# A transformer layer on one core: the blocks of the Strassen stage are split in one piece each, two masks and scores share their buffers with it, a bias is loaded ahead, and the last third product is gated ahead

## The chip, the cores and the metric

The kernel runs on one core of one Trainium2 chip. The core has a matrix engine (TensorE, in the profile PE, with its weight loads as PEld), a vector engine (VectorE, DVE), an activation engine (ScalarE, ACT), GpSimd (POOL) and a queue engine (SyncE, SP), and 16 DMA engines. The metric is the time of one execution on the device in microseconds (us); less is better. Before the change it is 780.21 us, the median of three runs from 778.95 to 781.56.

## The reference

One layer over 512 tokens of width 1024 in f32: an RMS norm whose scale and shift come from a second input `c`, two causal sparse attentions, a gated merge, an output projection, and a gated feed-forward part of inner width 2816. The change lies in the last part, and in the gate vector `gt_f` that multiplies it:

```python
mod = jax.nn.silu(c) @ w_mod[l] + b_mod[l]
sh_m, sc_m, gt_m, sh_f, sc_f, gt_f = [m[:, None, :] for m in jnp.split(mod, N_MOD, axis=-1)]
...
h = rms_norm(x, g_ffn_norm[l]) * (1.0 + sc_f) + sh_f
g_ff, u_ff = jnp.split(h @ w_gate_up[l], 2, axis=-1)
x = x + gt_f * ((jax.nn.silu(g_ff) * u_ff) @ w_down[l])
```

## The kernel before

**Numbers.** Every f32 matmul operand is split into a high part (a cast to a rounded f32 form, on ACT) and a low part (value minus high part, a subtraction on DVE). A product is three matmuls: high by high, high by low, low by high (`mm3`).

**Order.** The kernel is written as tasks. While it is built, a planner keeps a clock for each engine, holds the free times of every buffer in `free`, and issues the instructions of PE, ACT, DVE and POOL in the order that its clocks, the `slack` and the `rank` of a task give; that order is final. Each of these engines works through its own queue in order. All of these instructions pass one helper, so the profile gives them all line L110. DMAs issued by SP have lines of their own: L183 weights of the earlier stages, L1012 the bias rows, L1408 and L1423 `w_down`, L1446 the stored sums, L1486 and L1523 the output. POOL issues DMAs at L1245 (`pool_dma`). Buffers are named by tags: `st` holds arriving weights (three buffers), `H`, `O`, `K`, `wh`/`wl` hold high and low parts, `s`, `gu`, `pT`, `cg`, `g` hold f32 blocks, `psacc`, `pstr`, `pspv`, `pss` are accumulators.

**Gate vector.** `gtf_task` makes `gt_f` in two halves of 512 columns. For each half `mod_rows` lets DVE sum the rows of `w_mod` weighted by silu(c) into `cg` (SCALAR_TENSOR_TENSOR on `st`), makes its high part on ACT (`gu<-cg`) and its low part on DVE (`gu<-cg,gu`), then loads the bias over `cg` itself (L1012), sums over the partitions with two matmuls by a column of ones (`pstr<-gu,oner`), and adds the bias on DVE (`cg<-pstr,cg`). This runs beside the first matmuls of the gate and up projection.

**Down projection.** It is one level of Strassen's scheme in Winograd's form. The 2816 rows of `w_down` are 11 pairs of 256 rows (NPAIR = 11, here c0 to c10), and for each pair the weights are four blocks of 128 x 512. In the first half a pair gives 24 matmuls of 128x512: products M1, M6, M7, M5, each for two token tiles. `load_first_half` fetches two blocks in one `st` and a third in `pT` or `gu`; `split_first_half` forms three sums on DVE (T3, T2, T1), of which T2 goes to a buffer `s` and by POOL to memory, and `split_into` makes high and low parts, the pair of blocks in `st` as one 128x1024 operation. `homes` gives the buffers for the parts: by turns `wh`/`wl` or two `H`. Pair 10's activations are finished while c0 and c1 are multiplied (`s<-psacc`, `gu<-s`, then low parts `O<-s`, `O<-gu`). In the second half a pair gives 18 matmuls (M2, M3, M4), with block T4 formed from the stored sum (`gu<-st,gu` or `pT<-st,pT`); `second_task` brings half of each pair's activations back from memory into `O` or `K`. Pairs 9 and 10 come together in `end`.

**Output.** `shared_sums` and `share` add up the products that several output blocks share and gate them (`g<-g,cg`, then `V<-V,g`) during the second half. `settle` multiplies a finished accumulator by `gt_f` into `s`, adds it to the residual `V` and stores a block. At the end M4's accumulators are settled: the first token tile as 128x512, the second in two pieces of 256 columns in new accumulators.

Of the kernel before, what the change touches and what calls it, by code (L numbers as in the profile page):

```python
# [116 lines left out]
def layer(ctx, tc, x, vecs, w_mod, w_in, gvecs, w_br_dsa, w_br_moba, w_out, w_gate_up, w_down, cosh, sinh, cosi, sini, out):  # L117
# [11 lines left out]
    NB = {"H": 4, "O": 4, "K": 4, "V": 2, "g": 16, "gu": 2, "s": 3, "pT": 2, "cg": 2}  # L129
# [101 lines left out]
    cmask = cp.tile([P, S], F32, name="cmask")  # L231
# [577 lines left out]
    def index_queries(i):  # L809
# [22 lines left out]
        sc = cp.tile([P, w], F32, name=f"score{i}")  # L832
# [45 lines left out]
    def head(br, i, h):  # L878
# [46 lines left out]
        if not any(b == br for b, _, _ in heads):  # L925
            ready.add(f"attn{br}")
            done(vals["vb" if br else "va"], qk["qb" if br else "qa"], qk["kb" if br else "ka"])

# [78 lines left out]
    def mod_rows(acc, col0, tag):  # L1007

        yield from column_sums(col0, tag, acc)
        parts = yield from halves(acc)  # L1010
        r0 = 24 + col0 // P
        nc.sync.dma_start(acc.rearrange("p (a d) -> p a d", d=P), vecs[r0:r0 + 4].partition_broadcast(P))  # L1012
        arriving(acc, 512)
        yield parts + (room("pstr"), acc)
# [3 lines left out]
        ve.tensor_tensor(out=acc, in0=pg, in1=acc, op=ALU.add)  # L1018
        done(pg, *parts)

# [346 lines left out]
    def gtf_task():  # L1367
        yield "ffn0"
        for half in range(2):
            yield room("cg")  # L1370
            gtf.append(t("cg", [P, 512]))
            yield from mod_rows(gtf[half], 5 * D + half * 512, "st")
        ready.add("gtf")
# [37 lines left out]

    def block_tag():
# [14 lines left out]
    def split_first_half(loaded):  # L1427

        c, st, b = loaded
        yield st, b, room("s")  # L1430
        t2 = t("s", [P, 512])
        ve.tensor_tensor(out=b, in0=b, in1=st[:, 1], op=ALU.subtract)
        ve.tensor_tensor(out=t2, in0=b, in1=st[:, 0], op=ALU.add)
        ve.tensor_tensor(out=st[:, 1], in0=st[:, 1], in1=st[:, 0], op=ALU.subtract)
# [3 lines left out]
        places = [(h0, l0), (h1[:, 0], l1[:, 0]), (h1[:, 1], l1[:, 1])]  # L1438
        yield from split_into(places, [(st, st), (b, b), (t2, t2)])
        pool_dma(sums2[c], t2, out_of=t2)  # L1440
        done(st, b, t2)
        return {"B11": (h0[:, 0], l0[:, 0]), "T1": (h0[:, 1], l0[:, 1]), "T3": places[1], "T2": places[2]}, tiles
# [7 lines left out]
    def split_second_half(loaded):  # L1450
# [3 lines left out]
        ve.tensor_tensor(out=b, in0=st[:, 0], in1=b, op=ALU.subtract)  # L1454
        places, tiles = yield from homes(3)
# [18 lines left out]
    def settle(i, half, acc, cs=slice(0, 512), store=True):  # L1474

        pump(lambda: "gtf" in ready)
        need_room("s")
        tmp = t("s", [P, 512])
# [226 lines left out]
```

## Time and profile before

| | us |
|---|---|
| median of the runs | 780.21 |
| the profiled execution's own time | 780.61 |
| its span in the trace | 778.8 |
| PE busy in the span | 764.0 (98%) |
| DVE busy | 542.8 (70%) |
| ACT busy | 390.8 (50%) |
| POOL busy | 48.2 (6%) |

Of the profiled execution 1.8 us lie outside the span. Busy time of an engine is summed over its instructions; idle time is put down to the instruction whose semaphore came last. A row of the timeline has the start of a run of like instructions, their time together, the engine, the line, the operation, the tiles and a count, and in brackets the idle time before and what ended it. The granted clock is TensorE's: 1.00 is 2.4 GHz, and in a stretch with a lower number part of the time was at 1.2 GHz.

### The profile page before, as it was taken

To read this page: it belongs to the slowest core of one execution; us is meant where nothing else is said; L and a number is where in the kernel's file an instruction comes from. 1 tells how busy PE (TensorE), PEld (TensorE's weight loads), DVE (VectorE), ACT (ScalarE), POOL (GpSimd) and SP (SyncE) were. 2 spreads that over 40 slices of the span, in tenths; PEclk is the share of its full clock that TensorE was granted. 3 is DMA by queue.
4 is the path that set the end of the run, shared out by engine and by line. 5 is a ranking of instruction groups with operands and counts; after the bars stand their busy time and mean duration, and the time that the engine had idled before them with its cause. 6 is when DMAs were issued, how large, how long until landed. Compare 5 with 4: busy or idle time off the path is not lost.

```text
span 778.8 us, 10322 instructions
## 1 busy us (share of the span) xinstructions
PE 764.0 (98%) x3668; PEld 633.6 (81%) x3668; DVE 542.8 (70%) x1023; ACT 390.8 (50%) x824; POOL 48.2 (6%) x65
## 2 busy tenths in 40 slices
PE   7999999999999999999999999999999999899997
PEld 6887888888788878888889987788888888788886
DVE  6974889989699786248768257554544446897787
ACT  6763786779776747624446223233332233444340
POOL 2000012001111000000000000000000000111100
PEclk9999999999999999999999999999999999999999
DMA  9976352531135364334521186543334444489882
GB/s 310 339 227 221 84 180 71 182 108 55 52 87 197 98 216 150 123 108 148 168 90 30 54 257 208 184 134 127 106 120 149 140 131 166 167 278 354 307 294 82
DMA packets 84560, 126.60 MB, mean 163 GB/s; under 512 B 8976, under 2 KB 49240, under 8 KB 84508
## 3 DMA queue, kind: packets, MB, share of 16 engines
q1 hardware_dynamic: 80460, 105.75, 42.5%
q0 software_dynamic: 4048, 20.19, 7.7%
q8 instruction: 29, 0.48, 0.3%
q14 instruction: 23, 0.19, 0.1%
HBM read 112.28 MB, written 13.64 MB: 162 GB/s over the span
## 4 chain that ended last, share of the span: by engine, by line
PE 93%; DVE 2%; SPq 2%; DMA 1%; issue 1%; ACT 0%; ACTq 0%; DVEq 0%
PE psacc L110 60%; PE pstr L110 15%; PE pspv L110 9%; PE pss L110 8%; SPq L183 1%; DMA K<-in_w_mod_dram 1%; DVE s L110 1%; DMA cg<-in_vecs_dram 1%; SPq L212 0%; DVE V L110 0%; DVE H L110 0%; DVE O L110 0%; ACT H L110 0%; SPq L221 0%; DVE gu L110 0%
## 5 line engine op out<-in xcount | busy, mean ns | idle before, releaser
L110 PE MATMUL psacc<-H,wh 128*128 128x512 f32 x576 | 182.7, 398 | 0.0
L110 DVE TENSOR_TENSOR wl<-st,wh 128x1024 fp32r<-128x1024 f32 (+1 forms) x106 | 127.8, 1206 | 61.1 <-ACT wh L110 58.3
L110 ACT CAST wh<-st 128x1024 fp32r<-128x1024 f32 (+1 forms) x106 | 109.6, 1035 | 88.0 <-PE psacc L110 32.6
L110 PE MATMUL psacc<-wh,H 128*128 128x512 f32 x384 | 126.4, 400 | 0.9 <-ACT H L110 0.9
L110 PEld LDWEIGHTS psacc<-H,wh 128*128 128x128 f32 x576 | 106.0, 188 | 22.3 <-issue 2.1
L110 PE MATMUL psacc<-H,wl 128*128 128x512 f32 x288 | 112.4, 390 | 0.0
L110 PEld LDWEIGHTS psacc<-wh,H 128*128 128x128 f32 x384 | 72.0, 188 | 16.4 <-ACT H L110 1.4
L110 PE MATMUL psacc<-wl,H 128*128 128x512 f32 x192 | 71.0, 390 | 0.0
L110 PEld LDWEIGHTS psacc<-H,wl 128*128 128x128 f32 x288 | 54.1, 188 | 11.6
L110 PE MATMUL pstr<-H,wh 128*128 128x512 f32 (+1 forms) x176 | 54.4, 390 | 1.7 <-DVE cg L110 1.7
L110 POOL TENSOR_TENSOR m<-m,mhalf 128x4 f32<-128x4 f32 (+1 forms) x24 | 28.6, 1192 | 390.9 <-DVE m L110 357.0
L110 PEld LDWEIGHTS psacc<-wl,H 128*128 128x128 f32 x192 | 36.1, 188 | 6.8
L110 PEld LDWEIGHTS pstr<-H,wh 128*128 128x128 f32 (+1 forms) x176 | 32.2, 183 | 9.7 <-DVE cg L110 2.2
L110 PE MATMUL psacc<-O,wh 128*128 128x512 f32 x128 | 39.4, 389 | 0.0
L110 ACT ACTIVATE s<-s,att 128x256 f32<-128x256 f32 (+3 forms) x64 | 34.2, 562 | 4.0 <-DVE att L110 3.7
L110 PE MATMUL psacc<-H,O 128*128 128x256 f32 (+1 forms) x240 | 35.4, 305 | 0.0
L110 PE MATMUL pstr<-H,wl 128*128 128x512 f32 (+1 forms) x88 | 34.3, 390 | 0.0
L110 DVE TENSOR_TENSOR s<-psacc,s 128x512 f32<-128x512 f32 x12 | 8.3, 690 | 37.3 <-PE psacc L110 34.7
L110 PEld LDWEIGHTS psacc<-H,O 128*128 128x128 f32 x240 | 32.1, 191 | 1.9
L110 ACT CAST H<-st 128x1024 fp32r<-128x1024 f32 x14 | 14.8, 1055 | 34.7 <-PE psacc L110 26.7
L110 PEld LDWEIGHTS psacc<-O,wh 128*128 128x128 f32 x128 | 24.0, 188 | 5.0
L110 PE MATMUL psacc<-wh,K 128*128 128x512 f32 x82 | 26.1, 389 | 0.0
(290 smaller groups left out, 1442.7 us busy)
## 6 DMA issues: line engine op xcount, KB each, us to landing
st<-in_w_gate_up_dram SPq DMA_DIRECT2D x88, 256.0 KB, 3.6
st<-in_w_in_dram SPq DMA_DIRECT2D x36, 512.0 KB, 3.6
K<-in_w_mod_dram SPq DMA_DIRECT2D x12, 1024.0 KB, 6.4
st<-in_w_down_dram SPq DMA_DIRECT2D x22, 512.0 KB, 4.8
second<-O POOLq DMA_DIRECT2D x11, 768.0 KB, 5.3
K<-in_w_mod_dram SPq DMA_DIRECT2D x16, 512.0 KB, 6.1
K<-second POOLq DMA_DIRECT2D x6, 768.0 KB, 7.5
st<-in_w_in_dram SPq DMA_DIRECT2D x16, 256.0 KB, 4.2
```

Of the source, the lines that this page charges most:

```text
L110: inst = f(*args, **kw)
L183: last_dma[0] = nc.sync.dma_start(st[:, :, o:o + n], src.rearrange("(k p) n -> p k n", p=P))
```

## The change

- `split_first_half` no longer calls `split_into`. It issues, for each pair, the cast of the first block, the three sums in the order T3, T1, T2, the other three casts, and right behind, after one `yield`, the four low parts, each 128x512; the 128x1024 cast and subtraction become two of half the size. T2 may go to `sc` or `s`.
- A new tag `sc` with two buffers holds the causal mask and the scores of the last token tile, and, when attention is over, biases and T2.
- `mod_rows` with a `bias_tag` takes a buffer `sc` for the bias and loads it before the column sums; `gtf_task` uses it. The matmuls wait for the planner's time of the low part plus 1.0.
- For c9 and c10 `split_second_half` multiplies T4 by the first half of `gt_f`, so M4 of these pairs comes out gated. M4 of c0 to c8 is settled with a product as before, for both token tiles, after c8; the last M4 gets an accumulator of its own and `settle(..., gated=True)` adds it to `V` in one operation.
- `share` tasks get slack 3.0 and rank 2, `second_task` slack 8.0 and rank 0.

```diff
@@ -126,7 +126,7 @@
     pp = ctx.enter_context(tc.tile_pool(name="pp", bufs=1, space=PS))
     dp = ctx.enter_context(tc.tile_pool(name="dp", bufs=1, space=bass.MemoryType.DRAM))
 
-    NB = {"H": 4, "O": 4, "K": 4, "V": 2, "g": 16, "gu": 2, "s": 3, "pT": 2, "cg": 2}
+    NB = {"H": 4, "O": 4, "K": 4, "V": 2, "g": 16, "gu": 2, "s": 3, "pT": 2, "cg": 2, "sc": 2}
     uid = [0]
     last_dma = [None]
 
...
@@ -829,7 +829,7 @@
         yield tuple(qT)
         kT = idx["kT"]
         w = (i + 1) * P
-        sc = cp.tile([P, w], F32, name=f"score{i}")
+        sc = t("sc", [P, w]) if i == NT - 1 else cp.tile([P, w], F32, name=f"score{i}")
 
         def weigh(h, rl):
             if h == 0:
...
@@ -1004,19 +1006,29 @@
         landed[0] = max(ck.dma, ck.ready[sums.tensor.name][0]) + 9.0
         done(tile)
 
-    def mod_rows(acc, col0, tag):
-
+    def mod_rows(acc, col0, tag, bias_tag=None):
+
+        r0 = 24 + col0 // P
+
+        def load_bias(tile):
+            nc.sync.dma_start(tile.rearrange("p (a d) -> p a d", d=P), vecs[r0:r0 + 4].partition_broadcast(P))
+            arriving(tile, 512)
+
+        if bias_tag:
+            yield room(bias_tag)
+            load_bias(bias := t(bias_tag, [P, 512]))
         yield from column_sums(col0, tag, acc)
         parts = yield from halves(acc)
-        r0 = 24 + col0 // P
-        nc.sync.dma_start(acc.rearrange("p (a d) -> p a d", d=P), vecs[r0:r0 + 4].partition_broadcast(P))
-        arriving(acc, 512)
-        yield parts + (room("pstr"), acc)
+        if not bias_tag:
+            load_bias(bias := acc)
+        yield parts + (room("pstr"), bias, lambda: ck.ready[parts[1].tensor.name][0] + 1.0)
         pg = ps("tr")
         for n, part in enumerate(parts):
             te.matmul(pg, oner.to_broadcast([P, P]), part, start=n == 0, stop=n == 1)
-        ve.tensor_tensor(out=acc, in0=pg, in1=acc, op=ALU.add)
+        ve.tensor_tensor(out=acc, in0=pg, in1=bias, op=ALU.add)
         done(pg, *parts)
+        if bias_tag:
+            done(bias)
 
     gtm = []
     landed = [0.0]
@@ -1369,7 +1381,7 @@
         for half in range(2):
             yield room("cg")
             gtf.append(t("cg", [P, 512]))
-            yield from mod_rows(gtf[half], 5 * D + half * 512, "st")
+            yield from mod_rows(gtf[half], 5 * D + half * 512, "st", "sc")
         ready.add("gtf")
 
 
@@ -1409,6 +1421,9 @@
         arriving(st, 1024)
         return st
 
+    def earliest(*tags):
+        return lambda: min([min(free[tag]) for tag in tags if free[tag]], default=None)
+
     def block_tag():
 
         tags = [tag for tag in ("pT", "gu") if free[tag] and (tag == "pT" or f"stored{NPAIR - 1}" in ready)]
@@ -1427,19 +1442,26 @@
     def split_first_half(loaded):
 
         c, st, b = loaded
-        yield st, b, room("s")
-        t2 = t("s", [P, 512])
-        ve.tensor_tensor(out=b, in0=b, in1=st[:, 1], op=ALU.subtract)
-        ve.tensor_tensor(out=t2, in0=b, in1=st[:, 0], op=ALU.add)
-        ve.tensor_tensor(out=st[:, 1], in0=st[:, 1], in1=st[:, 0], op=ALU.subtract)
+        yield st, b, earliest("sc", "s")
+        t2 = t(min((tag for tag in ("sc", "s") if free[tag]), key=lambda tag: min(free[tag])), [P, 512])
         sums2[c] = dp.tile([P, 512], F32, name=f"sums{c}")
         places, tiles = yield from homes(4)
         (h0, l0), (h1, l1) = places
-        places = [(h0, l0), (h1[:, 0], l1[:, 0]), (h1[:, 1], l1[:, 1])]
-        yield from split_into(places, [(st, st), (b, b), (t2, t2)])
+        places = [(h0[:, 0], l0[:, 0]), (h0[:, 1], l0[:, 1]), (h1[:, 0], l1[:, 0]), (h1[:, 1], l1[:, 1])]
+        blocks = [st[:, 0], st[:, 1], b, t2]
+
+        se.copy(places[0][0], blocks[0])
+        ve.tensor_tensor(out=b, in0=b, in1=st[:, 1], op=ALU.subtract)
+        ve.tensor_tensor(out=st[:, 1], in0=st[:, 1], in1=st[:, 0], op=ALU.subtract)
+        ve.tensor_tensor(out=t2, in0=b, in1=st[:, 0], op=ALU.add)
+        for n in (2, 1, 3):
+            se.copy(places[n][0], blocks[n])
+        yield
+        for n in (0, 2, 1, 3):
+            ve.tensor_tensor(out=places[n][1], in0=blocks[n], in1=places[n][0].bitcast(F32), op=ALU.subtract)
         pool_dma(sums2[c], t2, out_of=t2)
         done(st, b, t2)
-        return {"B11": (h0[:, 0], l0[:, 0]), "T1": (h0[:, 1], l0[:, 1]), "T3": places[1], "T2": places[2]}, tiles
+        return dict(zip(("B11", "T1", "T3", "T2"), places)), tiles
 
     def load_second_half(c):
         st, b = rows_of(2 * c + 1), t(block_tag(), [P, 512])
@@ -1452,6 +1474,9 @@
         c, st, b = loaded
         yield st, b
         ve.tensor_tensor(out=b, in0=st[:, 0], in1=b, op=ALU.subtract)
+        if c >= NPAIR - 2:
+
+            ve.tensor_tensor(out=b, in0=b, in1=gtf[0], op=ALU.mult)
         places, tiles = yield from homes(3)
         (h0, l0), (h1, l1) = places
         places = [(h0, l0), (h1[:, 0], l1[:, 0])]
@@ -1471,17 +1496,20 @@
             pair_tiles[q] = [x]
             ready.add(f"second{q}")
 
-    def settle(i, half, acc, cs=slice(0, 512), store=True):
-
-        pump(lambda: "gtf" in ready)
-        need_room("s")
-        tmp = t("s", [P, 512])
+    def settle(i, half, acc, cs=slice(0, 512), gated=False, store=True):
+
         n = cs.stop - cs.start
-        ve.tensor_tensor(out=tmp[:, :n], in0=acc[:, :n], in1=gtf[half][:, cs], op=ALU.mult)
         cols = slice(half * 512 + cs.start, half * 512 + cs.stop)
         xs = x1[i // 2][:, i % 2, cols]
-        ve.tensor_tensor(out=xs, in0=xs, in1=tmp[:, :n], op=ALU.add)
-        done(tmp)
+        if gated:
+            ve.tensor_tensor(out=xs, in0=xs, in1=acc[:, :n], op=ALU.add)
+        else:
+            pump(lambda: "gtf" in ready)
+            need_room("s")
+            tmp = t("s", [P, 512])
+            ve.tensor_tensor(out=tmp[:, :n], in0=acc[:, :n], in1=gtf[half][:, cs], op=ALU.mult)
+            ve.tensor_tensor(out=xs, in0=xs, in1=tmp[:, :n], op=ALU.add)
+            done(tmp)
         if store:
             nc.sync.dma_start(ov[:, i, cols], xs)
 
@@ -1508,7 +1536,7 @@
             ve.tensor_tensor(out=c12, in0=acc, in1=kept["U2", tt], op=ALU.add)
             ve.tensor_tensor(out=c22, in0=acc, in1=kept["U3", tt], op=ALU.add)
             done(kept["U2", tt])
-            spawn(share(tt, c12, c22, kept["U3", tt]), slack=1.0, rank=3, on=(DVE,))
+            spawn(share(tt, c12, c22, kept["U3", tt]), slack=3.0, rank=2, on=(DVE,))
 
     def share(tt, c12, c22, u3):
         yield "gtf"
@@ -1565,7 +1593,7 @@
                 settle(tt, 1, acc)
             else:
                 pump(lambda: f"shared{tt}" in ready)
-                settle(2 + tt, 0, acc, store=tt == 0)
+                settle(2 + tt, 0, acc, store=False)
             if n != "M1":
                 done(acc)
 
...
@@ -1596,11 +1624,19 @@
                 for tt in range(2):
                     if (n, tt) == ("M4", 1):
                         continue
+                    if n == "M4":
+                        need_room("psacc")
+                        banks[n, tt] = ps("acc")
                     for q in (last - 1, last):
                         emptied_next[0] = q == last
-                        product(n, a, b, tt, q, held, q == last, banks[n, tt], skip=n == "M2")
+                        product(n, a, b, tt, q, held, q == last, banks[n, tt], start=n == "M4" and q != last,
+                                skip=n == "M2")
                     emptied_next[0] = False
-                    finish(n, tt)
+                    if n == "M4":
+                        settle(2 + tt, 0, banks[n, tt], gated=True)
+                        done(banks[n, tt])
+                    else:
+                        finish(n, tt)
                     step()
 
             n, a, b, _ = table[-1]
@@ -1610,7 +1646,7 @@
                 cs = slice(e, e + 256)
                 for q in (last - 1, last):
                     product(n, a, b, 1, q, held, q == last, acc, cs=cs, start=q != last, more=False)
-                settle(3, 0, acc, cs=cs)
+                settle(3, 0, acc, cs=cs, gated=True)
                 done(acc)
             leave(last - 1, last)
 
...
@@ -1652,7 +1689,7 @@
         for k2 in range(NK // 2):
             spawn(resident("w0", w0, gate_up_src(0, k2), 2, w0_hl, "attn0", "attn1", room("O")))
         spawn(gtf_task())
-        spawn(second_task())
+        spawn(second_task(), slack=8.0, rank=0, on=(DVE,))
         dve = (DVE,)
         spawn(columns_task(), slack=1.0, rank=3, on=dve)
         for i in range(1, NT):
```

The instructions of DVE in the first half, where c2 and c3 are split. In the kernel before, `pT_5969` and `st_5967` are c2's blocks, `pT_6029` and `st_6027` c3's, and the `O` rows are pair 10's activations:

```order
L110 TENSOR_TENSOR pT_5969<-pT_5969,st_5967 128x512
L110 TENSOR_TENSOR s_6064<-pT_5969,st_5967 128x512
L110 TENSOR_TENSOR st_5967<-st_5967 128x512
L110 TENSOR_TENSOR O_6057<-s_5999,O_6057 128x512
L110 TENSOR_TENSOR O_6057<-gu_6043,O_6057 128x512
L110 TENSOR_TENSOR O_6077<-s_6018,O_6077 128x512
L110 TENSOR_TENSOR O_6077<-gu_6044,O_6077 128x256
L110 TENSOR_TENSOR pT_6029<-pT_6029,st_6027 128x512
L110 TENSOR_TENSOR s_6101<-pT_6029,st_6027 128x512
L110 TENSOR_TENSOR st_6027<-st_6027 128x512
L110 TENSOR_TENSOR H_6070<-st_5967,H_6069 128x1024
```

The same place after, where `pT_5973` and `st_5971` are c2's blocks and `s_6009`, `s_6030` pair 10's activations:

```order
L110 TENSOR_TENSOR pT_5973<-pT_5973,st_5971 128x512
L110 TENSOR_TENSOR st_5971<-st_5971 128x512
L110 TENSOR_TENSOR s_6022<-pT_5973,st_5971 128x512
L110 TENSOR_TENSOR H_6040<-st_5971,H_6039 128x512
L110 TENSOR_TENSOR H_6040<-pT_5973,H_6039 128x512
L110 TENSOR_TENSOR H_6040<-st_5971,H_6039 128x512
L110 TENSOR_TENSOR H_6040<-s_6022,H_6039 128x512
L110 TENSOR_TENSOR gu_6081<-s_6009,s_6030 128x256
L110 TENSOR_TENSOR gu_6081<-s_6009 128x256
L110 TENSOR_TENSOR s_6009<-gu_6081,s_6009 128x256
L110 TENSOR_TENSOR gu_6082<-s_6030,s_6009 128x256
L110 TENSOR_TENSOR pT_6020<-pT_6020,st_6018 128x512
```

The four low parts of c2 stood behind c2's sums, four `O` rows and c3's sums; now they stand behind c2's sums alone.

PE in the gate and up projection, at the second half of the gate vector (`oner` is the column of ones; `wh_4690` and the `wh_4633` of the kernel before hold successive blocks of 256 weight rows, 24 matmuls each):

```order
L110 MATMUL psacc_4605<-H_3944,wh_4690 128x512
L110 MATMUL psacc_4605<-H_3946,wh_4690 128x512
L110 MATMUL psacc_4605<-H_3944,wl_4691 128x512
L110 MATMUL pstr_4769<-gu_4715,oner 128x512
L110 MATMUL pstr_4769<-gu_4716,oner 128x512
L110 MATMUL psacc_4607<-H_3944,wh_4690 128x512
L110 MATMUL psacc_4607<-H_3946,wh_4690 128x512
```

The same two matmuls after, where `wh_4634` is the block that was `wh_4633`:

```order
L110 MATMUL psacc_4610<-H_3944,wh_4634 128x512
L110 MATMUL psacc_4610<-H_3946,wh_4634 128x512
L110 MATMUL psacc_4610<-H_3944,wl_4635 128x512
L110 MATMUL pstr_4735<-gu_4712,oner 128x512
L110 MATMUL pstr_4735<-gu_4713,oner 128x512
L110 MATMUL psacc_4609<-H_3944,wh_4634 128x512
L110 MATMUL psacc_4609<-H_3946,wh_4634 128x512
```

The pair of matmuls by `oner` stands 24 matmuls earlier, and the rest keeps its order.

DVE at the very end, where `psacc_6571`, `pspv_6885` and `pss_6896` are the accumulators of the last M4:

```order
L110 TENSOR_TENSOR s_6881<-psacc_6571,cg_4418 128x512
L110 TENSOR_TENSOR V_3303<-V_3303,s_6881 128x512
L110 TENSOR_TENSOR s_6892<-pspv_6885,cg_4418 128x256
L110 TENSOR_TENSOR V_3303<-V_3303,s_6892 128x256
L110 TENSOR_TENSOR s_6903<-pss_6896,cg_4418 128x256
L110 TENSOR_TENSOR V_3303<-V_3303,s_6903 128x256
```

The same place after, with `psacc_6904`, `pspv_6913` and `pss_6922`:

```order
L110 TENSOR_TENSOR s_6890<-pspv_6589,cg_4593 128x512
L110 TENSOR_TENSOR V_3302<-V_3302,s_6890 128x512
L110 TENSOR_TENSOR s_6900<-pss_6595,cg_4593 128x512
L110 TENSOR_TENSOR V_3302<-V_3302,s_6900 128x512
L110 TENSOR_TENSOR V_3303<-V_3303,psacc_6904 128x512
L110 TENSOR_TENSOR V_3303<-V_3303,pspv_6913 128x256
L110 TENSOR_TENSOR V_3303<-V_3303,pss_6922 128x256
```

Three products by `cg` are gone from the last six rows; ahead of this piece, behind the low parts of c10, one settlement of a 128x512 accumulator has been added.

## Rows read from the trace of the kernel before

**Rows 1.** The page: the span, the busy time of each engine, and the chain of work that ended last, by engine.

```profile
span 778.8 us, 10322 instructions
...
PE 764.0 (98%) x3668; PEld 633.6 (81%) x3668; DVE 542.8 (70%) x1023; ACT 390.8 (50%) x824; POOL 48.2 (6%) x65
...
PE 93%; DVE 2%; SPq 2%; DMA 1%; issue 1%; ACT 0%; ACTq 0%; DVEq 0%
```

**Rows 2.** The waits of PE from 450 us to the end of the span: what waited for what, us in total, times, longest.

```profile
PE pstr L110 <- DVE H L110: 2.2, 1, 2.2
PE pstr L110 <- DVE cg L110: 1.7, 1, 1.7
PE pstr L110 <- DVE gu L110: 0.7, 1, 0.7
```

**Rows 3.** The timeline of PE in the first half of the Strassen stage: the first matmuls of c2 (675.87) and of c3 (685.33), and the wait between.

```profile
675.87 0.39 PE L110 MATMUL pstr<-H,g 128*128 128x512 f32 x1
678.42 2.50 PE L110 MATMUL pstr<-H,g 128*128 128x512 f32 x5 [2.17 <-DVE H L110]
...
685.33 0.39 PE L110 MATMUL pstr<-wh,g 128*128 128x512 f32 x1
```

**Rows 4.** Three stretches of 5 us: for each its start and end, its length, then busy time and count of PE, PEld, DVE, ACT and POOL, the granted clock, the share of the DMA engines and GB/s.

```profile
490.00:495.00 5.00, 3.27 (x15) 2.55 (x14) 3.50 (x7) 1.26 (x3) 0.00 (x0) 1.00 0.47 152
675.00:680.00 5.00, 2.83 (x10) 2.00 (x9) 4.96 (x8) 2.42 (x4) 1.61 (x3) 0.83 0.89 298
680.00:685.00 5.00, 5.00 (x20) 4.03 (x19) 4.63 (x8) 2.10 (x3) 1.08 (x2) 0.82 0.93 303
```

**Rows 5.** The timeline of DVE in the same stage: the evacuation of an accumulator and the idle time before it, c2's three sums (the first at 671.15), pair 10's low parts (from 673.08 to 674.89), c3's sums (from 675.22), c2's low part (677.15 and the next two).

```profile
665.89 0.69 DVE L110 TENSOR_TENSOR s<-psacc,s 128x512 f32<-128x512 f32 x1 [2.65 <-ACT s L110]
...
671.15 0.68 DVE L110 TENSOR_TENSOR pT<-pT,st 128x512 f32<-128x512 f32 x1
...
673.08 0.68 DVE L110 TENSOR_TENSOR O<-s,O 128x512 fp32r<-128x512 f32 x1
...
675.22 0.68 DVE L110 TENSOR_TENSOR pT<-pT,st 128x512 f32<-128x512 f32 x1
...
677.15 1.22 DVE L110 TENSOR_TENSOR H<-st,H 128x1024 fp32r<-128x1024 f32 x1
```

**Rows 6.** The timeline of DVE, SP, ACT and PE at the gate vector: the first half's bias is added at 467.36; for the second half the last `w_mod` load is issued at 476.18, the last two column sums begin at 482.58, the bias is issued at 486.93 and added at 491.17.

```profile
467.36 0.69 DVE L110 TENSOR_TENSOR cg<-pstr,cg 128x512 f32<-128x512 f32 x1 [2.66 <-DMA cg<-in_vecs_dram]
...
476.18 0.37 SPq L183 DMA_DIRECT2D st<-in_w_mod_dram  x1
482.58 1.54 DVE L110 SCALAR_TENSOR_TENSOR cg<-st,cs,cg 128x512 f32<-128x512 f32 x2 [2.46 <-DMA st<-in_w_mod_dram]
484.95 0.62 ACT L110 CAST gu<-cg 128x512 fp32r<-128x512 f32 x1
486.22 0.68 DVE L110 TENSOR_TENSOR gu<-cg,gu 128x512 fp32r<-128x512 f32 x1
485.82 0.40 PE L110 MATMUL pstr<-gu,oner 128*128 128x512 f32 x1
486.96 0.50 PE L110 MATMUL pstr<-gu,oner 128*128 128x512 f32 x1 [0.74 <-DVE gu L110]
486.93 0.34 SPq L1012 DMA_DIRECT2D cg<-in_vecs_dram  x1
491.17 0.69 DVE L110 TENSOR_TENSOR cg<-pstr,cg 128x512 f32<-128x512 f32 x1 [2.53 <-DMA cg<-in_vecs_dram]
491.92 0.73 PE L110 MATMUL pstr<-H,wh 128*128 128x512 f32 x2 [1.74 <-DVE cg L110]
```

**Rows 7.** The second half of the Strassen stage around c5 and c6: the load that c6's T4 waits for, DVE's T4 and low part for c6, PE's first matmuls of c5 (749.25) and c6 (753.33), the landing times of all `w_down` loads of L1408, and one stretch in the form of rows 4.

```profile
740.53 0.33 SPq L1408 DMA_DIRECT2D st<-in_w_down_dram  x1
749.37 0.69 DVE L110 TENSOR_TENSOR pT<-st,pT 128x512 f32<-128x512 f32 x1 [2.72 <-DMA st<-in_w_down_dram]
751.18 1.22 DVE L110 TENSOR_TENSOR H<-st,H 128x1024 fp32r<-128x1024 f32 x1
749.25 1.52 PE L110 MATMUL pstr<-H,O 128*128 128x512 f32 x6
753.33 1.52 PE L110 MATMUL pstr<-H,O 128*128 128x512 f32 x6
DMA to landing us min/median/max: 3.6/4.8/8.8
735.00:750.00 15.00, 15.00 (x68) 12.43 (x67) 11.57 (x18) 4.84 (x7) 1.06 (x2) 1.00 1.03 379
```

**Rows 8.** The end of the span: PE's last matmuls of M4 for c8 and its very last, and four of DVE's operations in the settlements, each of which is a product and a sum.

```profile
764.21 1.52 PE L110 MATMUL psacc<-H,O 128*128 128x512 f32 x6
773.68 0.28 PE L110 MATMUL pss<-wh,K 128*128 128x256 f32 x1
765.77 0.69 DVE L110 TENSOR_TENSOR s<-psacc,cg 128x512 f32<-128x512 f32 x1 [1.48 <-PE psacc L110]
767.13 0.69 DVE L110 TENSOR_TENSOR s<-pstr,cg 128x512 f32<-128x512 f32 x1
773.91 0.42 DVE L110 TENSOR_TENSOR s<-pspv,cg 128x256 f32<-128x256 f32 x1
775.15 0.42 DVE L110 TENSOR_TENSOR V<-V,s 128x256 f32<-128x256 f32 x1
```

More of the change, by code (lines that the diff above doesn't have):

```diff
@@ L230, in layer @@
     mhalf = cp.tile([P, 4], F32, name="mhalf")
-    cmask = cp.tile([P, S], F32, name="cmask")
+    cmask = t("sc", [P, S])
     identr = cp.tile([P, P], F32R, name="identr")
@@ L927, in head @@
             done(vals["vb" if br else "va"], qk["qb" if br else "qa"], qk["kb" if br else "ka"])
+            if not heads:
+                done(cmask, bias[NT - 1])
     heads = [(br, i, h) for br in (1, 0) for i in range(NT) for h in range(NH)]
@@ L1581, in part @@
                     acc = bank(n, tt, tags)
-                    ends = c == last if not second else c == last - 2 and (n, tt) == ("M4", 1)
+                    ends = c == last if not second else c == last - 2 and n == "M4"
                     emptied_next[0] = ends
@@ L1631, in layer @@
         free.update({"ps" + tag: [start] * n for tag, n in NPB.items()})
+        taken("sc", cmask)
         for n, tile in enumerate([cosd, sind, csi, gains]):
```

## The prediction

> **What bounds the kernel now.** The page first: PE is busy 764.0 of 778.8 us and holds 93% of the chain that ended last [rows 1]. So a change gains only what PE spends waiting, what it spends at a lower clock, or what follows its last matmul. The waits of PE from 450 us on are three, 2.2, 1.7 and 0.7 us [rows 2]; the change touches each. Read in the timeline, the 2.2 us fall between two matmuls of c2 [rows 3], and the stretches around and behind it show a granted clock of 0.83 and 0.82, while the stretch with the 1.74 us wait keeps 1.00 [rows 4]. The other two waits lie at the gate vector's second half [rows 6]. At the end DVE, not PE, is last: PE's last matmul ends at 773.96 and DVE's last sum at 775.57 [rows 8]. Of the profiled execution's 780.61 us, 778.8 are the span and 1.8 lie outside; I sum against the 780.61. The median of the runs is 0.4 lower, 780.21, so the forecast is given on that scale.
>
> **Part 1, the split of the first half.** In the second half 18 matmuls take 4.08 us (749.25 to 753.33) [rows 7], so the 24 of a pair in the first half take 5.44. But c2 takes 9.46 (675.87 to 685.33) [rows 3]: 4.02 too much, 2.17 of it the wait and the rest the low clock behind it. The wait is for DVE: c2's low part, ready to go by its operands once c2's sums end about 673, starts at 677.15, behind pair 10's low parts and c3's sums [rows 5]. In the new order nothing stands between c2's sums and its four low parts. By hand, with before's durations: a 128x512 operation is 0.68 and the next starts 0.6 later; three sums take 1.93 (671.15 to 673.08) and four low parts 4 x 0.6. c1's low parts now stand ahead of `s<-psacc`, where DVE idled 2.65 us [rows 5], so the two evacuations of accumulators start about 666.5, c2's sums about 667.7, and its low parts end about 672.1. PE wants them at 675.9: 3.8 us to spare. Pair 10's four operations of 128x256 follow, 0.42 each [rows 8], 1.6 in all, so c3 is ready about 678.1 (wanted 681.3) and c4 about 682.4 (wanted 686.8). From there DVE needs 4.3 per pair against PE's 5.44, and pair 10's low parts (2.1) fit in between.
>
> Added: two low parts of 128x512 for one of 128x1024, 2 x 0.6 against 1.14 by steps, some 0.1 per pair on DVE, and a cast more on ACT; both lie beside PE while the slack above holds. c0's `st` is freed later than before, since one of its casts waits for a `wh` buffer: about 662, if c1's sums and low parts are done by 666.5. Its next load is c3's, with sums at about 673.7; landings take 3.6 to 8.8 us [rows 7]. The value I take is the whole 4.0. It is bounded by 0 (a wait of the same size elsewhere) and 4.2.
>
> **Part 2, the gate vector.** Gone: the bias is loaded over `cg` only at 486.93 and holds the last addition until 491.17 [rows 6], for which PE waits 1.74. With the bias in `sc` long before, that wait goes. But the pair of matmuls by `oner` now stands 24 matmuls earlier, so PE is there at 485.82 - 5.44 = 480.4, and the `w_mod` load, which landed at 482.58 after 6.4 us, cannot be late any more. Its issue waits for a buffer of DVE's; in the new order DVE frees it two `O` rows sooner and no longer idles 2.66 us for the first half's bias (at 467.36). I put the issue at 473 (471.5 to 474.1), the landing at 479 (477.5 to 480.5), two column sums 1.54, cast 0.62, low part 0.68 and some latency behind it: the second matmul can go about 482, against 480.6. New wait about 1.3 (0 to 2.9) for 0.74 + 1.74 = 2.48. I take a gain of 1.2, bounded by -0.4 and 2.5. Behind the waiting pair on PE stands only gate and up work, whose weights are there.
>
> **Part 3, the second half.** Work is the same but for two products of 0.69 for c9 and c10 and a new order of `share`. PE reaches it 5.2 us earlier, so c6 is wanted at 748.1 instead of 753.33, and its low part was done at 752.40 because the `st` load, issued 740.53, had 8.8 us to land [rows 7]. The loads move too: their buffers are freed by DVE and PE, which are both earlier. With the new order I get slack of about 2.3, 2.8 and 1.7 us for c4, c5 and c6, and over 3 from c7. Cost 0; cover gone, c6 costs what its load lacks.
>
> The Trainium skill speaks against this: "DMA: Bandwidth & Descriptors", section "Specifications", gives about 358 GB/s from HBM for a core. The trace has 379 GB/s over 15 us here [rows 7], so the measurement decides; by the page's figure those bytes would take an estimated 15.9 us, 0.9 more, still inside c6's 1.7, and the sum stays. The same page, "Queues, rings and completion order", says each DMA engine takes turns between the queues that have work, so the earlier POOL reads slow SP's loads; no row here shows its price apart from the 3.6 to 8.8 us that loads took.
>
> **Part 4, the end.** Before, DVE works through products and sums of 1.36 each (765.77 to 767.13), then two halves, and ends 1.61 after PE [rows 8]. Now the first accumulator of c8's M4 can start about 0.7 sooner (its six matmuls of 764.21 end in the middle), six pairs of 1.36 follow, then one sum of 0.69 and two of 0.42 without products: 765.1 + 8.16 + 0.6 + 0.35 + 0.42 = 774.6 on before's clock, 0.9 to 1.0 sooner. It cannot be under 773.96 + 0.42, which bounds the gain at 1.2; the lower bound is 0.4, if the new first pair waits for `s`. I take 0.9.
>
> **Sum.** 4.0 + 1.2 + 0 + 0.9 = 6.1. 780.61 - 6.1 = 774.5 for a profiled execution, 780.2 - 6.1 = 774.1 on the median's scale.
>
> **Rivals.**
> A. *The gate vector's wait only changes its cause.* The load lands at 480.5 and PE idles 2.9 in one piece, longer than the 2.17 that was followed by the low clock. Then 0.4 is lost instead of 1.2 won: 775.7, and with some 1.85 us of low clock as behind c2 (4.02 - 2.17), 777.6. For: the landing took 6.4 us before, and nothing here shows the same load landing faster. Against: DVE's 2.66 us of idle time ahead of it goes [rows 6]. The Trainium skill, "TensorE: Matmul & The Clock Gate", section "HAM oscillation — how this bites in real kernels", says that waits for data throttle the engine again; by that rule A has its second part. This trace has it so behind 2.17 us of waiting, and not behind 0.74 and 1.74, which is why A's two times both stand.
> B. *The wait at c2 comes back at another pair.* DVE is busy 4.96 of 5 us there [rows 4] and the change adds to it. If half of the 4.0 stays, 776.1; if all, 778.1, which is within 0.3% of before. For: the casts on ACT and DVE go to and fro for each pair. Against: 3.8, 3.2 and 4.4 us of slack, and 0.1 per pair added.
> C. *The weights of the second half do not come sooner* (the other side). DMA is full from 735 to 750. If c6's load lands when it did, its low part is done at 752.4 against 748.1: 4.3 lost, and by the low clock another 1.85, in all 6.15, which is the whole gain: 780.2. If it lands more than 2.3 us later, because output stores now stand together ahead of it on SP and POOL reads beside it, the kernel is slower, some 783. With a stall s it loses s + 1.85; for slower by 2.3 that must be 8.4, so s is 6.6 and c6's data 8.2 us behind my estimate. Against: the loads are released by DVE and PE, which are both ahead, and from 675 to 685 DMA has some room left (0.89 and 0.93) [rows 4].
> D. *The new order does not do what it says*: low parts follow sums by construction, so only the casts could undo it; that is B.
>
> **How the numbers follow.** All parts as summed: 0.62 (772.6 to 775.3). A: 0.16. B: 0.13. C: 0.09, half of it slower by over 0.3%. 0.3% is 2.3 us, about what a measurement of this kernel can tell from no change. Faster (under 777.9): 0.62, 0.15 of A, 0.07 of B, 0.84 in all; same: 0.01 of A, 0.06 of B, 0.04 of C, 0.11; slower: 0.05. The range goes from 772.4, where the gains reach their upper bounds together (4.2 + 2.5 + 1.2), to 777.7, past A and half of B.
>
> **What would show it.** Right: no PE wait on DVE H after 670 us and a clock of 1.00 through the first half, c2 at 5.44; one PE wait near 480 of 0.5 to 2 us on `gu` and none on `cg`; DVE's last sum 0.5 to 0.8 behind PE's last matmul; no wait of PE between 720 and 770. Wrong: a wait on H or `wl` at c1, c3 or c4; a PE wait of over 2.5 us near 480 with a lower clock behind it; DVE waiting on `st<-in_w_down` right ahead of a PE wait at c5 to c7.

## The result, and the profile after

The changed kernel takes 773.08 us (median of four runs, 771.89 to 773.69) against 779.79 us beside it; the ratio is 0.9909 with a 95% interval from 0.9887 to 0.9931, so it is 5.4 to 8.8 us faster. The forecast was 774.1 us, in a range from 772.4 to 777.7. The profiled executions differ by more: 771.89 against 780.61, spans of 770.1 and 778.8. Where these 8.7 us lie, and which part of them is not the change's, is told below.

The head of the page and the chain that ended last, for the changed kernel, to hold against [rows 1]:

```profile
span 770.1 us, 10321 instructions
...
PE 762.7 (99%) x3668; PEld 633.7 (82%) x3668; DVE 543.9 (71%) x1035; ACT 394.4 (51%) x835; POOL 48.3 (6%) x65
...
PE 95%; SPq 2%; DVE 1%; DMA 1%; issue 0%; ACT 0%; ACTq 0%
```

All waits of PE in its span. The three of [rows 2] are gone, and what is left lies in the first 450 us:

```profile
PE pstr L110 <- DMA pT<-in_vecs_dram: 2.6, 1, 2.6
PE psacc L110 <- ACT H L110: 0.9, 2, 0.7
PE pstr L110 <- DMA K<-in_w_mod_dram: 0.2, 1, 0.2
```

The timeline at c2, PE first, then DVE with c2's first sum and its first and last low part, for [rows 3, 5]; and two stretches in the form of [rows 4]:

```profile
672.33 1.52 PE L110 MATMUL pstr<-H,g 128*128 128x512 f32 x6
...
677.77 0.39 PE L110 MATMUL pstr<-wh,g 128*128 128x512 f32 x1
...
664.04 0.68 DVE L110 TENSOR_TENSOR pT<-pT,st 128x512 f32<-128x512 f32 x1
...
665.97 0.68 DVE L110 TENSOR_TENSOR H<-st,H 128x512 fp32r<-128x512 f32 x1
...
667.77 0.69 DVE L110 TENSOR_TENSOR H<-s,H 128x512 fp32r<-128x512 f32 x1
...
670.00:675.00 5.00, 5.00 (x24) 4.14 (x23) 4.96 (x9) 3.41 (x6) 0.54 (x1) 1.00 0.48 164
675.00:680.00 5.00, 5.00 (x23) 4.14 (x23) 4.97 (x9) 2.47 (x4) 0.54 (x1) 1.00 0.78 248
```

c2 takes 5.44 us (672.33 to 677.77). Its low parts end at 668.46, 3.9 us before PE needs them; before, they began 1.3 us after PE had begun c2 [rows 3, 5]. DVE is as busy as it was (4.96 and 4.97 of 5). What has changed at c2 is what stands ahead of its low parts, and their size; the experiments tell the two apart.

The second half of the gate vector, for [rows 6]: the last `w_mod` load, the last column sums, the low part, the two matmuls by the column of ones, and the addition of the bias.

```profile
472.61 0.37 SPq L183 DMA_DIRECT2D st<-in_w_mod_dram  x1
477.15 1.54 DVE L110 SCALAR_TENSOR_TENSOR cg<-st,cs,cg 128x512 f32<-128x512 f32 x2 [0.50 <-DMA st<-in_w_mod_dram]
479.43 0.69 DVE L110 TENSOR_TENSOR gu<-cg,gu 128x512 fp32r<-128x512 f32 x1 [0.74 <-ACT gu L110]
479.95 0.73 PE L110 MATMUL pstr<-gu,oner 128*128 128x512 f32 x2
482.91 0.68 DVE L110 TENSOR_TENSOR cg<-pstr,sc 128x512 f32<-128x512 f32 x1
```

The load is there 4.5 us after its issue, not 6.4, the low part is ready at 480.1, and PE does not wait.

The second half around c6, for [rows 7]: a load on SP, two T4 and two low parts on DVE, PE's first matmuls of c6; then the end, for [rows 8]:

```profile
736.68 0.34 SPq L1420 DMA_DIRECT2D st<-in_w_down_dram  x1
740.72 0.69 DVE L110 TENSOR_TENSOR pT<-st,pT 128x512 f32<-128x512 f32 x1
742.99 0.69 DVE L110 TENSOR_TENSOR gu<-st,gu 128x512 f32<-128x512 f32 x1 [0.39 <-DMA st<-in_w_down_dram]
743.60 1.22 DVE L110 TENSOR_TENSOR H<-st,H 128x1024 fp32r<-128x1024 f32 x1
744.74 0.69 DVE L110 TENSOR_TENSOR H<-pT,H 128x512 fp32r<-128x512 f32 x1
745.77 1.52 PE L110 MATMUL pstr<-H,O 128*128 128x512 f32 x6
...
757.53 0.69 DVE L110 TENSOR_TENSOR s<-psacc,cg 128x512 f32<-128x512 f32 x1 [1.30 <-PE psacc L110]
765.50 0.68 DVE L110 TENSOR_TENSOR V<-V,psacc 128x512 f32<-128x512 f32 x1
766.12 0.28 PE L110 MATMUL pss<-wh,O 128*128 128x256 f32 x1
766.44 0.42 DVE L110 TENSOR_TENSOR V<-V,pss 128x256 f32<-128x256 f32 x1
```

c6's low part is ready at 744.82, 0.95 us before PE. DVE's last sum ends 0.46 behind PE's last matmul, where it was 1.61.

In [rows 7] and in the prediction the load of 740.53 and the T4 of 749.37 of the kernel before stand as c6's. They are c7's. A T4 stays in its buffer, `pT` or `gu`, until its low part is made, so the buffers tell whose it is. In the kernel before:

```profile
743.01 0.69 DVE L110 TENSOR_TENSOR gu<-st,gu 128x512 f32<-128x512 f32 x1 [0.71 <-DMA st<-in_w_down_dram]
752.32 0.69 DVE L110 TENSOR_TENSOR H<-gu,H 128x512 fp32r<-128x512 f32 x1
754.66 0.69 DVE L110 TENSOR_TENSOR wl<-pT,wh 128x512 fp32r<-128x512 f32 x1
757.41 0.39 PE L110 MATMUL pstr<-wh,O 128*128 128x512 f32 x1
```

The `pT` of 749.37 goes into `wl` at 754.66, and the pair that PE multiplies from `wh` and `wl`, at 757.41, is c7. c6's T4 is the `gu` of 743.01. Its low parts came only at 751.18, though ACT's cast of its `st` was done at 746.19, because c7's T4 stood ahead of them in DVE's queue and waited 2.72 us for c7's load. That is the fault of c2 once more, hidden by 0.9 us of slack. In the changed kernel the order is the same (c7's T4 is the row at 742.99), and c7's load is there 6.3 us after its issue, not 8.8.

Between the two traces the 8.7 us divide so: 0.43 up to the first matmul by `oner` (463.56 to 463.13), ahead of the places that the change is about; 2.9 from there to c0's first matmul (664.77 to 661.45); 4.24 from c0's first matmul to the end of PE's last (109.19 to 104.95); 1.15 from there to DVE's last sum.

### The profile page after: what moved, and what is told of

Read it like the earlier page. It is cut to its first block, busy times and chain, and to the rows that moved or that the text cites. A ratio compares the mean times of both kernels' runs of the same rounds, so it can differ in the third digit from the quotient of the medians.

```text
span 770.1 us, 10321 instructions
## 1 busy us (share of the span) xinstructions
PE 762.7 (99%) x3668; PEld 633.7 (82%) x3668; DVE 543.9 (71%) x1035; ACT 394.4 (51%) x835; POOL 48.3 (6%) x65
## 4 chain that ended last, share of the span: by engine, by line
PE 95%; SPq 2%; DVE 1%; DMA 1%; issue 0%; ACT 0%; ACTq 0%
PE psacc L110 62%; PE pstr L110 15%; PE pspv L110 9%; PE pss L110 9%; SPq L183 1%; DMA K<-in_w_mod_dram 1%; SPq L212 1%; DVE V L110 1%; DVE s L110 1%; SPq L221 0%; ACT gu L110 0%; ACT H L110 0%; SPq L205 0%; ACT acol L110 0%; ACT mcol L110 0%
## 5 line engine op out<-in xcount | busy, mean ns | idle before, releaser
L110 PE MATMUL psacc<-H,O 128*128 128x256 f32 (+1 forms) x234 | 33.8, 303 | 0.0
L110 ACT CAST H<-st 128x512 fp32r<-128x512 f32 (+1 forms) x21 | 16.1, 766 | 20.8 <-PE psacc L110 20.3
L110 ACT ACTIVATE s<-psacc 128x512 f32<-128x512 f32 x12 | 7.1, 596 | 37.2 <-PE psacc L110 37.2
```

The costliest lines, as they stand in the source:

```text
L110: inst = f(*args, **kw)
```

## The experiments

Eleven runs were made beside the kernel before, two of them of kernels already seen; the medians of the kernel before are 779.9, 779.9 and 780.0 us. The 95% intervals reach 1.2 to 2.1 us to each side, so the times separate the large parts only. For the small ones there is one trace each.

**The parts, each alone.** The first has only the new `split_first_half` (with T2 in `s`), the second only `sc` and the early bias, the third only the gated T4 and the new end.

```diff
-        yield st, b, earliest("sc", "s")
-        t2 = t(min((tag for tag in ("sc", "s") if free[tag]), key=lambda tag: min(free[tag])), [P, 512])
+        yield st, b, room("s")
+        t2 = t("s", [P, 512])
```

> The kernel before with the new split_first_half alone (T2 in s only; no sc, old bias, old end, old ranks). Theory (the wait at c2 was a queue on DVE, and the low clock behind it was its consequence): PE's wait on DVE H (2.17) is gone, the granted clock is 1.00 through the first half, c2 takes 5.44, and the time falls by 4.0 to 4.3 us. Rival (the low clock has another cause): only the wait goes, the time falls by about 2.2 and a stretch near 0.82 stays. Rival (the wait moves to another pair): within 1 us of before.

776.08 us (ratio 0.9943, from 0.9923 to 0.9964), 3.8 below before, with an interval from 2.8 to 6.0 that leaves both rivals out. c2 takes 5.44 and the clock is 1.00. The theory of the queue holds; that the low clock must follow from the wait does not, as the next runs show.

```diff
-            yield from mod_rows(gtf[half], 5 * D + half * 512, "st")
+            yield from mod_rows(gtf[half], 5 * D + half * 512, "st", "sc")
```

> The kernel before with sc and the bias loaded ahead alone. Theory (both PE waits at the gate vector's second half hung on the bias load and on the late column sums behind it): PE waits there fall from 2.48 to under 0.3, as in the changed kernel, and the time falls by 2.2 to 2.5 us; the last w_mod load is issued about 472.6 and lands in under 5 us. Rival (my estimate in the prediction): the load takes about 6 us to land, a wait of 1.3 stays on PE and the time falls by 1.2.

777.63 us (0.9968, from 0.9945 to 0.9992), 2.3 below. PE's waits from 450 us on are now one, the one at c2; two stretches behind it follow:

```profile
PE pstr L110 <- DVE H L110: 2.2, 1, 2.2
675.00:680.00 5.00, 3.67 (x16) 3.05 (x17) 4.96 (x8) 2.60 (x4) 1.00 (x3) 1.00 1.01 379
680.00:685.00 5.00, 5.00 (x24) 4.14 (x23) 4.97 (x8) 2.83 (x5) 1.00 (x2) 1.00 0.97 291
```

The wait at c2 is the same 2.2 us as in [rows 2], but the clock behind it is 1.00, and c2 takes 7.95, not 9.46. So 1.5 of the 4.0 us that I had counted for c2 are not always there.

```diff
-                settle(3, 0, acc, cs=cs)
+                settle(3, 0, acc, cs=cs, gated=True)
```

> The kernel before with the gated T4 of c9 and c10 and the new settlement of M4 alone. Theory: PE's work is the same, DVE's last sum comes 0.4 to 0.5 instead of 1.6 us behind PE's last matmul, the time falls by 1.1 us. Rival: the two products added for c9 and c10 delay DVE's low parts and PE waits for them at the last pairs; then 0 or slower.

779.77 us (0.9992, from 0.9974 to 1.0011): the expected 1.1 did not come. The rival had the time, but not the way: at the last pairs PE waits for no low part. The rows are the weight load of the last piece on PE, and the third and the second last of DVE's sums:

```profile
772.88 0.41 PEld L110 LDWEIGHTS pss<-H,K 128*128 128x128 f32 x3 [0.30 <-DVE s L110]
773.47 0.68 DVE L110 TENSOR_TENSOR V<-V,psacc 128x512 f32<-128x512 f32 x1
774.07 0.41 DVE L110 TENSOR_TENSOR V<-V,pspv 128x256 f32<-128x256 f32 x1
```

DVE comes out of the low parts of c10 only at 765.59 and starts the settlements without a pause, so it is late through the end: the last piece of M4 waits for DVE to empty `pss` (from the last pairs' first matmul to the last takes 8.75 instead of 8.39), and DVE ends 0.95 behind PE. By the trace 0.66 is won and 0.36 given back.

> The changed kernel beside the three parts on the same chip. If the parts add up, its gain is the sum of theirs, about 7.8 us (4.2 + 2.5 + 1.1). If the parts hide each other, its gain differs from that sum by over 1.5 us.

772.29 us (0.9902, from 0.9877 to 0.9927), 7.6 below; the parts alone sum to 3.8 + 2.3 + 0.1 = 6.2. The surplus is within the intervals, but the end is a place where the parts do need each other, which the next runs show.

**The low clock, and what makes the end pay.** The kernel before once more, the changed kernel with the old split, the changed kernel with the old ranks, and the kernel before with the new end and the new ranks:

```diff
-            spawn(share(tt, c12, c22, kept["U3", tt]), slack=3.0, rank=2, on=(DVE,))
+            spawn(share(tt, c12, c22, kept["U3", tt]), slack=1.0, rank=3, on=(DVE,))
-        spawn(second_task(), slack=8.0, rank=0, on=(DVE,))
+        spawn(second_task())
```

> The kernel before once more, for its trace. In the traces so far the low clock stood behind the wait at c2 in one execution of the kernel before, and in two of its variants (bias_only, end_only) it stood in the first 20 us instead, with the same 2.17 us wait at c2 and a clock of 1.00 behind it. Theory (the wait at c2 is always there, the low clock behind it comes in some executions only): a wait of 2.1 to 2.2 at c2, and from c0's first matmul to PE's last either 109.2 us with the low clock or about 107.6 without. Rival (the low clock belongs to the wait): 109.2 again.

779.40 us (0.9992, from 0.9971 to 1.0013). The same wait, 2.2 us, a clock of 1.00 behind it, c0 to PE's last matmul 107.62. So the wait belongs to the order, the low clock to the execution:

```profile
675.00:680.00 5.00, 2.79 (x13) 1.99 (x12) 4.93 (x8) 2.09 (x3) 1.61 (x3) 1.00 0.97 324
```

> The changed kernel with the old split_first_half; everything else as changed. Theory: the queue on DVE is back, PE waits 2.1 to 2.2 on DVE H at c2, c0's first matmul to PE's last takes 107.5 (109.2 with the low clock) instead of 104.95, and the time is 2.6 to 4.2 us above the changed kernel, 775 to 776.5. Rival (the sc buffers or the new ranks are what relieved DVE): no wait at c2 and the time of the changed kernel.

777.74 us (0.9953, from 0.9934 to 0.9971), against 772.29 and 773.08 for the changed kernel; that is above the expected 775 to 776.5, and 2.1 under the kernel before, about what the early bias gives alone. PE waits 2.2 on DVE H again, this time with the low clock:

```profile
675.00:680.00 5.00, 3.02 (x9) 2.41 (x10) 4.96 (x9) 2.09 (x3) 0.38 (x2) 0.80 0.99 339
```

c2 takes 9.56, c0 to PE's last 109.29. Over the seven traces with this wait c2 takes 7.94 to 7.95 in four and 9.46 to 9.56 in three: the wait and the small gaps around it cost 2.5, and the low clock 1.5 to 1.6 more in three of seven.

> The changed kernel with the old slack and rank of share and second_task. Theory (the gated end pays only where DVE is ahead of PE at the last pairs, and the earlier share work or the earlier first half puts it ahead): if the ranks are needed, DVE's last sum comes 0.9 behind PE's last and PE loses some 0.5 at the end as in end_only, 1.0 us above the changed kernel. Rival (the earlier first half is enough): within 0.3 us of the changed kernel, 0.46 behind PE.

773.62 us (0.9908, from 0.989 to 0.9927), 1.3 and 0.5 above the two measurements of the changed kernel, which the intervals do not separate. In the trace DVE no longer waits for the first accumulator of M4 but is behind it, and its last sum comes 0.96 behind PE:

```profile
758.00 0.68 DVE L110 TENSOR_TENSOR wl<-pT,wh 128x512 fp32r<-128x512 f32 x1
758.61 0.68 DVE L110 TENSOR_TENSOR s<-psacc,cg 128x512 f32<-128x512 f32 x1
...
767.50 0.41 DVE L110 TENSOR_TENSOR V<-V,pss 128x256 f32<-128x256 f32 x1
```

By this trace the ranks are needed for the whole gain at the end, even with the earlier first half. They are worth 0.6 us: 0.50 of DVE's last sum and 0.09 that PE loses, where I had expected it to lose 0.5.

> The kernel before with the gated end and the new ranks, no new split, no early bias. Theory (the ranks make room for the two added products): DVE's last sum 0.46 behind PE's last instead of 0.95 in end_only, the time 1.0 to 1.2 under before. Rival (only the earlier first half makes room): as end_only, 0.95 behind and the time within 0.5 of before.

779.58 us (0.9985, from 0.9969 to 1.0), which can't tell 0 from 1.1. The trace can:

```profile
770.38 0.69 DVE L110 TENSOR_TENSOR s<-psacc,cg 128x512 f32<-128x512 f32 x1 [1.01 <-PE psacc L110]
```

DVE waits 1.01 us for M4's first accumulator, PE's last pairs take 8.39, and DVE ends 0.46 behind PE. So the new ranks make the room for the two added products without the earlier first half. Which of the two, `share`'s or `second_task`'s, no run tells.

**Order or size, and the landing of the load.**

```diff
-        for n in (2, 1, 3):
-            se.copy(places[n][0], blocks[n])
+        for h, v in ((places[2][0], b), (h0, st), (places[3][0], t2)):
+            se.copy(h, v)
         yield
-        for n in (0, 2, 1, 3):
-            ve.tensor_tensor(out=places[n][1], in0=blocks[n], in1=places[n][0].bitcast(F32), op=ALU.subtract)
+        for (h, l), v in (((h0, l0), st), (places[2], b), (places[3], t2)):
+            ve.tensor_tensor(out=l, in0=v, in1=h.bitcast(F32), op=ALU.subtract)
```

> The changed kernel with the blocks of st cast and subtracted whole again (128x1024), sums and low parts still in one piece. Theory (the place in DVE's queue relieved PE, not the size of the pieces): no PE wait in the first half, every pair 5.44, the time of the changed kernel within 0.5 us; DVE works about 0.1 per pair less. Rival (the halves matter, since the cast and the low part of the first block can go before T1 is there): a PE wait on H comes back at c1 or c2.

775.87 us (0.9932, from 0.9908 to 0.9955), about 3 above the changed kernel, and neither side had it right: every pair of the first half takes 5.44, and PE waits in the second half. DVE in the first half, then DVE and PE in the second:

```profile
668.97 1.23 DVE L110 TENSOR_TENSOR H<-st,H 128x1024 fp32r<-128x1024 f32 x1 [0.51 <-ACT H L110]
...
739.39 0.69 DVE L110 TENSOR_TENSOR pT<-st,pT 128x512 f32<-128x512 f32 x1 [1.33 <-DMA st<-in_w_down_dram]
741.27 0.50 PE L110 MATMUL pstr<-wl,K 128*128 128x512 f32 x1 [1.22 <-DVE wl L110]
```

The whole block can be cast only when T1 is there, the cast takes 1.05, and DVE stands for it 0.5 us in every pair, since the low part is now next in its queue. That adds up: DVE ends c10's split at 714.55, against 708.10 in the changed kernel, starts the second half late, and c0, c1, c2 and c4 of the second half take 4.50, 4.71, 4.18 and 5.61 instead of 4.08. From c0 of the first half to PE's last it is 107.63, 2.7 over. The largest loss, 1.5 at c4, has a load in it too: c4's low parts stand behind c5's T4, which waits 1.33 us for its load (739.39), as c6's stood behind c7's in the kernel before.

```diff
-        yield from split_into(places, [(st, st), (b, b), (t2, t2)])
+        yield from split_into(places, [(st, st[:, 0]), (st, st[:, 1]), (b, b), (t2, t2)])
```

> The kernel before with its order, only that casts and low parts of the two blocks in st are two of 128x512 each. Theory: the wait at c2 stays, 2.2 to 2.4 us, c2 takes 7.9 to 8.1 (or 9.5 with the low clock), the time is that of before. Rival (the size of the pieces mattered): the wait falls by over 0.5.

778.75 us (0.9978, from 0.9953 to 1.0003). The wait falls to 1.5, the rival's side by a little, but c2 still takes 7.67, since PE's next products then wait for the other parts one by one:

```profile
677.80 1.43 PE L110 MATMUL pstr<-H,g 128*128 128x512 f32 x5 [1.50 <-DVE H L110]
```

So the order does the work at c2, and the halves make it affordable. Whole blocks with the low part of T3 first, while ACT still casts the pair in `st`, might do the same; no run tried it.

```diff
-        pool_dma(second_acts[gi], x, out_of=x)
+        if gi == 1:
+            second_acts[gi] = second_acts[0]
+        else:
+            pool_dma(second_acts[gi], x, out_of=x)
```

> The kernel before without one transfer: the second half of pair 1's activations is not stored (768 KB by POOL, issued 0.4 us ahead of the last w_mod load), and pair 0's are read in its place. In four traces with that store ahead the load was waited for until 5.75 to 6.4 us after its issue, in five with the load 1.2 us ahead of it until 4.25 to 4.7. Theory (the load shares the DMA engines with the store): it is there 4.2 to 5.0 us after its issue, PE's 0.7 us on gu at the second half of the gate vector is gone, and its wait on cg is under 1.0. Rival (the landing depends on the two gate and up loads ahead of it on its own queue): 5.8 to 6.4 as before.

778.33 us (0.9972, from 0.9945 to 0.9998).

```profile
475.81 0.37 SPq L183 DMA_DIRECT2D st<-in_w_mod_dram  x1
480.14 1.54 DVE L110 SCALAR_TENSOR_TENSOR cg<-st,cs,cg 128x512 f32<-128x512 f32 x2 [0.31 <-DMA st<-in_w_mod_dram]
490.17 0.73 PE L110 MATMUL pstr<-H,wh 128*128 128x512 f32 x2 [1.14 <-DVE cg L110]
```

The load is there after 4.33 us, and the wait on `gu` is gone; the one on `cg` is 1.14, over the 1.0 that I had expected. In the traces with the store 0.4 us ahead the load took 5.75 to 6.45 us in five and 7.47 in one. So the store by POOL, beside the load, cost it 1.4 us or more.

## Why the prediction was right, step by step

**What bounds the kernel**: right. Each of PE's three waits went, and the time went with them. How far the sum met is in part luck, as its terms show.

**Part 1** (4.0): the mechanism is right, shown by the split alone and by taking it away. The term is right for the trace that I read (4.24), but it is not one number. The wait and the small gaps around it cost 2.5 to 2.7 in all seven traces that have it. The 1.85 that I put down to the low clock were 1.5 of low clock and 0.3 of gaps, and the low clock, which I took to follow the wait, came in three of the seven. A forecast on the medians' scale should have counted about 3.3 (2.6, and 1.55 in three of seven). One reading was short: c2's low part was not ready when its sums ended, about 673, but when ACT's cast of `st` did, at 674.30. The queue held it for 2.85 us from there. "0.1 per pair added" by the halves had the wrong sign: whole blocks in the new order cost 2.7 in the second half. I counted DVE's work, and not DVE's wait for the cast.

**Part 2** (1.2, a new wait of 1.3): the mis-sized term. The issue was right (473 against 472.61), the landing was not (479 against 477.15): the 6.4 us that I carried over from [rows 6] had the store of 768 KB in them, and in the new order the load goes 1.2 us ahead of that store. The wait left is 0 to 0.2 in the traces with the early bias, so the gain is 2.3 in the median of that part alone and 2.5 to 2.9 by the first two traces. The 2.48 is not one number either: PE's waits there were 1.65 in the second trace of the kernel before, and 0.9 to 3.4 in the variants with the old bias.

**Part 3** (0): the cost is right, on a slack of 0.95 at c6 where I had 1.7, but c6 was not covered by its own load: the load of 740.53 is c7's, and c6's low part waited for it only through DVE's queue. Rival C had its place right: it is what `whole_blocks` ran into, by a late DVE, and at c4 by DVE standing for a load.

**Part 4** (0.9): 1.15 in the trace. The added first pair did not wait for `s`. That the gain hangs on the new ranks of `share` and `second_task`, which I had given no weight of their own, the traces of the two runs on the ranks show: without them 0.3 to 0.6 us of it are left.

**The sum** (6.1) is 0.6 under the first measurement's 6.7 and 1.5 under the second's 7.6: too little for the gate vector, too much for the clock, and the two offset each other. The record lists the mean granted clock of each execution to three places, which sets the clock apart. At 1.000 ten executions of the kernel before have a median of 778.0 us and four of the changed one 772.0; at 0.997 it is 779.9 and 773.7. So at one and the same clock the change is worth 6.0 to 6.2 us. What goes beyond comes from how often the clock was low: 0.995 or under in 25 of 82 executions before, and in none of ten after. That fits a low clock that can no longer follow a wait at c2, but which stretch was slow the list does not say. (The lower end of the range, 780.2 less 7.9, is 772.3 and not 772.4.) Of the rivals, A fell by its landing time, 4.5 us; B stayed out by 3.9 us of slack at c2, where I had 3.8.

## What to carry to other kernels

Where the busiest engine waits for a helper that is itself always busy, look at what stands ahead of the awaited instruction in the helper's queue before counting its work: moving four instructions forward was worth 2.5 us at c2, with DVE as busy as before. What awaits a load should not stand ahead of what is ready: its wait becomes that of everything behind it (c6 in the kernel before, c4 in `whole_blocks`). When a chain of casts and subtractions is put in one piece across two engines, cut the pieces so that neither engine stands for the other; 0.5 us per pair came out again as 2.7 us, in the stage behind. And a price read from one trace, a landing time or a stretch of low clock, has its neighbours in it: look who shares the queue or whether a second trace shows it again.

## What was not expected of the hardware

Behind the same wait of 2.2 us of PE the granted clock fell to its lower level in part of the next 10 us in three traces (0.83 and 0.82; 0.80 and 0.86; 0.98 and 0.68) and stayed at 1.00 in four, which makes 1.5 to 1.6 us of one and the same order. The Trainium skill, "TensorE: Matmul & The Clock Gate", section "HAM oscillation — how this bites in real kernels", counts such a loss behind each of a kernel's waits for data, which are longer than this one; these traces have it behind some. What decides it in an execution no run here shows. In five of the thirteen traces the clock was low in the first 20 us too (a mean of 0.91 in four, 0.81 in `end_ranks`), and at 1.00 there in the others.

A load of 512 KB on SP's queue took 4.3 us without the store of 768 KB by POOL, 4.25 to 4.8 when it was issued 1.2 us ahead of the store (six traces), and 5.75 to 7.5 when it was issued 0.4 us behind it (six traces). This agrees with the taking of turns between queues that the Trainium skill tells of in "DMA: Bandwidth & Descriptors", section "Queues, rings and completion order".
